# Strassen-form products in six gated tiles of an FFN's up projection, and a later place for the down projection's operands

## The chip, the cores and the metric

The kernel runs on one core of one Trainium2 chip. The metric is the device time of one execution in microseconds (us), as the median of several runs.

## The reference

One layer of a streaming encoder on 544 rows: 512 of a prompt and 32 of a sample. Two attention mixers come first; they and their projections are the same, instruction for instruction, in both kernels. What the change touches is the last line of the layer, the feed-forward part:

```python
# D_MODEL 1024, D_FF 2816, CONV_W 3
x = x + w_down( gelu(a) * b ),  [a | b] = causal depthwise conv3( RMSNorm(x) @ w_up )

u = h @ w_up                                   # h = RMSNorm(x), u has 2*D_FF columns
c = conv_b + conv_w[0]*up[0:t] + conv_w[1]*up[1:1+t] + conv_w[2]*up[2:2+t]
a, g = split(c, 2)
return (gelu(a) * g) @ w_down, up[-(CONV_W-1):]
```

The last two rows of u of prompt and sample are an output, too (the convolution's state).

## The kernel before

**Layout.** Everything is held transposed: features on the 128 partitions, the 544 rows of x as columns. The columns go in two halves of 272 (s = 0 and 1), the 1024 features of x in eight blocks k. For float32 accuracy each operand is split in a high part and a remainder (hi by a rounding copy to fp32r on ScalarE, lo = x - hi on VectorE), and each block product is three matmuls of 128x128 by 272 columns into PSUM: hi by xh, hi by xl, lo by xh. All of them go through one helper, line 86.

**Up projection (the loop over `gate_order`).** w_up has 44 tiles of 128 rows; value tile i and gate tile 22+i make one gated tile, of which there are 22. `conv` does one of the 44: 2 halves by 8 blocks by 3 = 48 matmuls, so 96 a gated tile. Each weight tile (128x1024, 512 KB) is loaded, cast to `w_hi` on ScalarE (L204) and split to `w_lo` on VectorE (L205), three tiles ahead of its use; `w_raw`, `w_hi` and `w_lo` have two buffers each. Behind a half, VectorE multiplies the PSUM sum by the norm's 1/rms and writes it to `u` (L939). Behind the second half GpSimd copies the state's columns, ScalarE starts the convolution (L945), VectorE adds its two other taps (L946, L951), with two small GpSimd instructions between them for the columns where the sample begins. A value tile then gets Gelu (L988, ScalarE), a gate tile is multiplied in (L993, VectorE).

**Operands of the down projection.** The first 6 gated tiles in order (16 to 21, "rest") are split to hi and lo as they are made. The other 16 go in 8 pairs: `make_pair` (L964 to L981) forms sums and differences of the two tiles' halves (VectorE) and splits these. Five of the eight pairs are made between the up projection's tiles, the last three after it.

**Down projection.** The rest part (L1049 to L1061) runs 8 output tiles of 36 matmuls over the 6 rest tiles, each followed by two additions into x1 (L1059). The pair part runs over the pairs, with 7 products of 6 matmuls where the plain form has 8; `sums` makes its weight operands on VectorE (L1018 to L1021, L1025) and ScalarE (L1024), ten ahead.

**Order.** The program is written tile by tile, and a scheduler that simulates a timeline sets each engine's order from it; weight preparation is issued with a priority offset (`LATER`), so that it yields to other ready work. PSUM has eight banks: `psd` with three and `psa` with five, used in turn.

## Time and profile before

| | us |
|---|---|
| median of 3 runs | 921.65 |
| lowest and highest | 920.37, 924.04 |
| the profiled execution | 921.02 |
| its span in the trace | 919.2 |

The span is what the instruction records cover; 1.82 us of the execution lie around it. Busy times are sums of instruction durations. An engine starts its next instruction before the record of the last one ends, so on VectorE and ScalarE the distance from start to start, where rows stand back to back, says what an instruction takes from its engine; the duration is an upper bound. For the matmuls the page's durations overlap, and the distance comes from two events a known number of matmuls apart.

Three stretches of the trace matter: the up projection (from about 531 us, with the norm's factor ready at 543, to 795.6), the rest part (to 831.5) and the pair part (to 916).

### The profile page before, as it was taken

Reading aid. Unit: us, or ns where it says so; the run is one execution under the profiler, and the core shown is the slowest. Engines: PE = TensorE matmul, PEld = TensorE weight load, DVE = VectorE, ACT = ScalarE, POOL = GpSimd, SP = SyncE. Lnnn points to the kernel's source line nnn. Section 1 sums busy time; section 2 is a strip of 40 time slices with the busy share of each in tenths; the row PEclk is TensorE's granted clock in tenths of the full one; section 3 lists DMA queues with packets and bytes.
Section 4 is the critical chain, followed back from the end, with each engine's and each line's share of the span. In section 5 each row is a group of like instructions: output and inputs, shape, how many; then the busy total and the mean of one; then the engine's idle time right before and its main releaser. Section 6 shows DMA issues by size and latency. Waiting matters only on the chain.

```text
span 919.2 us, 18903 instructions
## 1 busy us (share of the span) xinstructions
PE 895.1 (97%) x7085; PEld 881.3 (96%) x7085; DVE 720.0 (78%) x1470; ACT 540.5 (59%) x1283; POOL 378.2 (41%) x577
## 2 busy tenths in 40 slices
PE   7979999999999999999999999999999999999998
PEld 6979999989989999999999999999999999999998
DVE  7798867777988888997856568677787776886996
ACT  5668887778878677777663244334444433534542
POOL 4625548466867767765541213222222221100100
PEclk9999999999999999999999999999999999999999
DMA  7222133312344343343415222222222222232342
GB/s 223 90 89 87 53 96 92 112 58 82 109 133 125 113 145 106 124 126 120 134 47 189 83 79 92 93 92 80 82 93 92 92 90 76 93 107 78 117 146 67
DMA packets 40012, 94.38 MB, mean 103 GB/s; under 512 B 4944, under 2 KB 16240, under 8 KB 39920
## 3 DMA queue, kind: packets, MB, share of 16 engines
q1 hardware_dynamic: 39920, 93.17, 31.9%
q8 instruction: 56, 0.92, 0.4%
q14 instruction: 36, 0.29, 0.1%
HBM read 80.48 MB, written 7.10 MB: 95 GB/s over the span
## 4 chain that ended last, share of the span: by engine, by line
PE 78%; DVE 8%; ACT 3%; POOL 3%; issue 2%; DMA 0%; DVEq 0%; POOLq 0%; ACTq 0%
PE ps L86 75%; PE ps L90 3%; DVE q L449 1%; ACT p L488 1%; DVE w_lo L205 1%; DVE p L504 1%; POOL p L496 1%; DVE zn L425 1%; DVE s L255 1%; DVE t_b L320 1%; POOL t_sql L417 1%; DVE k L434 0%; POOL z L424 0%; DVE xl L328 0%; DMA k<-k 0%
## 5 line engine op out<-in xcount | busy, mean ns | idle before, releaser
L86 PE MATMUL ps<-xh,w_lo 128*128 128x272 f32 x1536 | 445.3, 291 | 5.6 <-DVE w_lo L205 5.6
L86 PE MATMUL ps<-xh,w_hi 128*128 128x272 f32 x1536 | 444.5, 291 | 2.8 <-ACT z L415 1.7
L86 PE MATMUL ps<-xl,w_hi 128*128 128x272 f32 x1536 | 444.5, 290 | 0.4 <-DVE xl L328 0.3
L86 PEld LDWEIGHTS ps<-xh,w_lo 128*128 128x128 f32 x1536 | 290.3, 189 | 7.0 <-DVE w_lo L205 6.5
L86 PEld LDWEIGHTS ps<-xh,w_hi 128*128 128x128 f32 x1536 | 290.1, 189 | 4.6 <-ACT z L415 1.9
L86 PEld LDWEIGHTS ps<-xl,w_hi 128*128 128x128 f32 x1536 | 290.6, 189 | 1.5 <-DVE xl L328 1.1
L205 DVE TENSOR_TENSOR w_lo<-w_raw,w_hi 128x1024 fp32r<-128x1024 f32 (+2 forms) x112 | 143.0, 1277 | 32.6 <-ACT w_hi L204 18.7
L202 POOL TENSOR_SCALAR w_hi<-w_raw 128x1024 fp32r<-128x1024 f32 (+2 forms) x62 | 67.0, 1082 | 92.9 <-PE ps L86 69.2
L496 POOL TENSOR_SCALAR p<-p,rc 128x256 f32<-128x256 f32 (+3 forms) x128 | 74.7, 601 | 41.3 <-DVE rc L494 37.9
L204 ACT CAST w_hi<-w_raw 128x1024 fp32r<-128x1024 f32 x50 | 52.6, 1051 | 64.8 <-issue 36.0
L86 PE MATMUL ps<-s,w_hi 128*128 128x272 f32 x448 | 84.0, 288 | 0.0
L488 ACT ACTIVATE p<-p,nm 128x256 f32<-128x256 f32 (+3 forms) x128 | 65.4, 513 | 28.0 <-DVE nm L485 27.9
L942 POOL TENSOR_SCALAR state_u<-u 128x2 f32<-128x2 f32 x44 | 17.1, 389 | 145.5 <-DVE u L939 145.5
L86 PE MATMUL ps<-s 128*128 128x272 f32 (+1 forms) x483 | 71.3, 293 | 1.7 <-DVE s L374 1.7
L86 PEld LDWEIGHTS ps<-s,w_hi 128*128 128x128 f32 x448 | 70.0, 188 | 0.0
L939 DVE TENSOR_TENSOR u<-ps,rstd 128x272 f32<-128x272 f32 x88 | 38.5, 440 | 39.6 <-PE ps L86 36.9
L86 PEld LDWEIGHTS ps<-s 128*128 128x128 f32 x483 | 65.0, 190 | 2.2 <-DVE s L374 1.7
L86 PE MATMUL ps<-s,w_lo 128*128 128x272 f32 x224 | 63.7, 288 | 0.0
L86 PE MATMUL ps<-k,q 128*128 128x256 f32 (+2 forms) x256 | 52.2, 308 | 3.3 <-DMA k<-k 1.6
L417 POOL TENSOR_TENSOR t_sql<-t_sq,t_sqh 128x272 fp32r<-128x272 f32 x52 | 52.6, 1012 | 3.7
L424 POOL TENSOR_TENSOR z<-z,t_y 128x272 f32<-128x272 f32 x52 | 42.7, 822 | 21.9 <-ACT t_y L317 19.9
L515 DVE TENSOR_TENSOR pt_l<-ps,pt_h 128x512 fp32r<-128x512 f32 (+1 forms) x80 | 45.6, 602 | 5.5 <-ACT pt_h L514 4.3
(164 smaller groups left out, 1627.3 us busy)
## 6 DMA issues: line engine op xcount, KB each, us to landing
w_raw<-in_w_in SPq DMA_DIRECT2D x50, 512.0 KB, 3.4
w_raw<-in_w_up SPq DMA_DIRECT2D x44, 512.0 KB, 3.3
w_raw<-in_w_pair SPq DMA_DIRECT2D x16, 512.0 KB, 3.3
k<-k SPq DMA_DIRECT2D x40, 128.0 KB, 2.3
bias<-in_rel SPq DMA_DIRECT2D x16, 256.0 KB, 2.9
w_raw<-in_w_out SPq DMA_DIRECT2D x8, 512.0 KB, 3.4
s<-in_x SPq DMA_DIRECT2D x15, 272.0 KB, 5.7
w_raw<-in_w_down SPq DMA_DIRECT2D x6, 512.0 KB, 3.3
```

Source lines behind the costliest of these rows:

```text
L86: return self.nc.tensor.matmul(out, lhsT=lhsT, rhs=rhs, **kw)
L90: return self.nc.tensor.transpose(out, src, ident)
L202: G.tensor_scalar(hi[:, c], raw[:, c], 1.0, 1.0, ALU.mult, ALU.mult)
L204: nc.scalar.copy(hi[:, c], raw[:, c])
L205: V.tensor_tensor(lo[:, c], raw[:, c], rr(hi)[:, c], ALU.subtract)
L417: G.tensor_tensor(sql, sq, rr(sqh), ALU.subtract)
L424: G.tensor_tensor(z, z, y, ALU.mult)
L488: act(p[:, sl], p[:, sl], AF.Exp, bias=nm[:, t:t + 1], accum_out=sm[:, t:t + 1])
L496: G.tensor_scalar(p[:, sl], p[:, sl], rc[:, t:t + 1], 1.0, ALU.mult, ALU.mult)
L515: V.tensor_tensor(l[:, :n], ps[:, :n], rr(h)[:, :n], ALU.subtract)
L939: V.tensor_tensor(u[:, 2 + c0:2 + c0 + cn], ps, rstd2[:, c0:c0 + cn], ALU.mult)
L942: G.tensor_scalar(state_u[:, m, 0:2], u[:, NP:NP + 2], 1.0, 1.0, ALU.mult, ALU.mult)
```

## The change

**Shared tiles.** Six of the 22 gated tiles (numbers 7, 9, 11, 13, 15, 17 in the order) no longer run as a value tile and a gate tile. They are taken together as a 2 by 2 product of blocks: {value, gate} by {even blocks k, odd blocks k} by {left half, right half of the columns}. A Strassen form makes it from 7 block products instead of 8. Each is 4 blocks by 3 matmuls = 12, so a shared tile has 84 matmuls for 96. Its weights are four loads of 128x512 (256 KB) in place of two of 512 KB, four sums (VectorE) and seven splits of 128x512 (ScalarE and VectorE). Three products are copied from PSUM on ScalarE and four results are formed on VectorE into the two `u`.

**Rows that carry the norm.** Sums of left and right columns need the factor 1/rms in the rows themselves. So `with_norm` makes scaled rows of x1 (eight, during up tiles 1 to 4), and `form` makes the four sums a pair of blocks needs (during tiles 6 to 9). From up tile 6 on, the plain tiles run on the scaled rows as well, and their sum leaves PSUM by a copy on ScalarE (L960) instead of a multiplication on VectorE.

**Operands later.** The six rest splits, which came tile by tile, come together at gated tile 17; one pair is made after each of the tiles 18 to 21, and the other four in the rest part.

The core of the diff (lines that are left out handle buffers and the host's layout of the weights; the body of `conv_end` is the old code behind `evac`):

```diff
-EARLY = 5
 UNITS = PAIRS // 2
 H = T // 2
+SHARED = (7, 9, 11, 13, 15, 17)
+AHEAD_UP = 6
+TAKE = {17: 6, 18: 1, 19: 1, 20: 1, 21: 1}
 ...
+RESCALE2 = 6
 ...
-    for i in gate_order:
-        sources += [a["w_up"][i], a["w_up"][GT + i]]
+    for n, i in enumerate(gate_order):
+        if n not in SHARED:
+            sources += [a["w_up"][i], a["w_up"][GT + i]]
 ...
+    def conv_end(m, u, done, own):
 ...
+        done(c)
+    def conv(m, n, done, own):
         u = us[n % 2]
 
         def evac(s, c0, cn, ps):
-            V.tensor_tensor(u[:, 2 + c0:2 + c0 + cn], ps, rstd2[:, c0:c0 + cn], ALU.mult)
-            if s == 0:
-                return
 ...
-            done(c)
+            if n < RESCALE2:
+                V.tensor_tensor(u[:, 2 + c0:2 + c0 + cn], ps, rstd2[:, c0:c0 + cn], ALU.mult)
+            else:
+                nc.scalar.copy(u[:, 2 + c0:2 + c0 + cn], ps)
+            if s == 1:
+                conv_end(m, u, done, own)
         dense(evac, psa if n % 2 else psd)
 ...
+    scaled_x, plain, forms = [], [], []
+    def with_norm(k):
+        x = fp.tile([128, T], F32, name="s")
+        V.scalar_tensor_tensor(x, x1[k], col("n2", k), rstd2, ALU.mult, ALU.mult)
+        h, l = (fp.tile([128, T], F32R, name="s") for _ in range(2))
+        split(h, l, x)
+        scaled_x.append(x)
+        plain.append((h, l))
+    def sums_of(v1, v2, t13, t24):
+        b11, b12, b21, b22 = (v[:, c:c + H] for v in (v1, v2) for c in (0, H))
+        V.tensor_tensor(t13[:, :H], b11, b12, ALU.subtract)
+        V.tensor_tensor(t13[:, H:], b12, b22, ALU.subtract)
+        V.tensor_tensor(t24[:, :H], b22, t13[:, :H], ALU.add)
+        V.tensor_tensor(t24[:, H:], b21, t24[:, :H], ALU.subtract)
+    def form(j):
+        t13, t24 = (fp.tile([128, T], F32, name="s") for _ in range(2))
+        sums_of(scaled_x[2 * j], scaled_x[2 * j + 1], t13, t24)
+        ops = {}
+        for e, (names, t) in enumerate(((("t1", "t3"), t13), (("t2", "t4"), t24))):
+            h, l = (xp.tile([128, T], F32R, name=f"x{p}{2 * j + e}") for p in "hl")
+            split(h, l, t)
+            for i, name in enumerate(names):
+                ops[name] = tuple(x[:, i * H:i * H + H] for x in (h, l))
+        for e, names in enumerate((("b11", "b12"), ("b21", "b22"))):
+            for i, name in enumerate(names):
+                ops[name] = tuple(x[:, i * H:i * H + H] for x in plain[2 * j + e])
+        forms.append(ops)
+    def sums_up():
+        for n in range(len(SHARED)):
+            wc, wd, wa, wb = (fp.tile([128, T], F32, name="s")[:, :512] for _ in range(4))
+            for e, w in enumerate((wc, wd, wa, wb)):
+                load(w, a["w_shared"][n, :, 512 * e:512 * e + 512])
+            s1, s2, s3, s4 = (fp.tile([128, T], F32, name="s")[:, :512] for _ in range(4))
+            def both(x):
+                h, l = (fp.tile([128, T], F32R, name="s")[:, :512] for _ in range(2))
+                split(h, l, x)
+                ready_up.append((h, l))
+            both(wa)
+            yield
+            V.tensor_tensor(s1, wc, wd, ALU.add)
+            V.tensor_tensor(s2, s1, wa, ALU.add)
+            both(s2)
+            yield
+            both(s1)
+            yield
+            V.tensor_tensor(s3, wc, wa, ALU.add)
+            both(s3)
+            yield
+            both(wb)
+            yield
+            V.tensor_tensor(s4, s2, wb, ALU.add)
+            both(s4)
+            yield
+            both(wd)
+            yield
+    ready_up, used_up = [], []
 ...
+    def ahead_up(n):
+        while len(ready_up) < len(used_up) + n:
+            with tc.high_priority(LATER):
+                if next(making_up, 0) == 0:
+                    break
+    def shared(m1, m2, nth, done1, done2, own):
+        pool = psa if nth % 2 else psd
 ...
+        ba, bb, bc = (bank(pool)[:, :H] for _ in range(3))
+        p0, q1, e = (ft.tile([128, 272], F32, name=x) for x in ("t_y", "t_b", "t_v"))
+        (y11, y12), (y21, y22) = ((u[:, 2:2 + H], u[:, 2 + H:2 + T]) for u in us)
+        tt = V.tensor_tensor
+        def product(ps, name, first):
+            ahead_up(AHEAD_UP)
+            h, l = ready_up[len(used_up)]
+            used_up.append(name)
+            for j in range(KC // 2):
+                ks = slice(128 * j, 128 * j + 128)
+                xh, xl = forms[j][name]
+                mm(ps, lhsT=h[:, ks], rhs=xh, start=first and j == 0, stop=False, skip_group_check=True)
+                mm(ps, lhsT=h[:, ks], rhs=xl, start=False, stop=False, skip_group_check=True)
+                mm(ps, lhsT=l[:, ks], rhs=xh, start=False, stop=j == KC // 2 - 1, skip_group_check=True)
+        product(bb, "b11", True)
+        nc.scalar.copy(p0, bb)
+        product(ba, "t2", True)
+        nc.scalar.copy(q1, ba)
+        product(bb, "t1", False)
+        nc.scalar.copy(e, bb)
+        product(ba, "t3", False)
+        tt(y22, ba, e, ALU.subtract)
+        product(bc, "b21", True)
+        tt(y11, bc, p0, ALU.add)
+        product(bb, "b22", False)
+        tt(y12, bb, q1, ALU.subtract)
+        conv_end(m1, us[0], done1, own)
+        product(ba, "t4", False)
+        tt(y21, ba, p0, ALU.subtract)
+        conv_end(m2, us[1], done2, fp)
 ...
+    gated, made = [], [0]
+    def take(n):
+        for _ in range(n):
+            j = made[0]
 ...
+            else:
+                j = REST + 2 * (j - REST)
+                if j + 1 >= len(gated):
+                    return
+                make_pair(gated[j], gated[j + 1])
+            made[0] += 1
 ...
+        own = gp if n <= max(SHARED) else fp
 
         def value(c, part=part):
             act(c, c, AF.Gelu)
             part.append(c)
 
-        def gate(c, part=part, n=n):
+        def gate(c, part=part):
             v = part[0]
             V.tensor_tensor(v, v, c, ALU.mult)
-            if n < REST:
-                h, l = home(), home()
-                split(h, l, v)
-                rest.append((h, l))
-                return
-            late.append(v)
-            if n % 2 and len(pairs) < EARLY:
-                make_pair(*late)
-                late.clear()
-        conv(i, 2 * n, value)
-        conv(GT + i, 2 * n + 1, gate)
+            gated.append(v)
+        if n in SHARED:
+            shared(i, GT + i, SHARED.index(n), value, gate, own)
+        else:
+            for e, (m, done) in enumerate(((i, value), (GT + i, gate))):
+                conv(m, tile_no, done, own if e == 0 else fp)
+                if 1 <= tile_no <= 4:
+                    with_norm(2 * tile_no - 2)
+                    with_norm(2 * tile_no - 1)
+                if tile_no == RESCALE2 - 1:
+                    moving[:] = plain
+                if RESCALE2 <= tile_no < RESCALE2 + 4:
+                    form(tile_no - RESCALE2)
+                if tile_no >= RESCALE2 + 4 and len(used_up) < 7 * len(SHARED):
+                    ahead_up(AHEAD_UP)
+                tile_no += 1
+        if n >= max(SHARED):
+            take(TAKE.get(n, 1))
     nc.sync.dma_start(out=o["conv"], in_=state_u)
-    for j in range(0, len(late), 2):
-        make_pair(late[j], late[j + 1])
+    take(GT)
```

What this does to the engines' orders is shown at three places. Names ending in numbers are buffers of one run of the program: `ps` is PSUM, `s` a row buffer, `u0` and `u1` the two inputs of the convolution.

**TensorE where up tile 7 ends.** Up tiles are numbered from 0 here. Before, tile 7 (`w_hi_8415`) ends with its right half; tile 8 (`w_hi_8486`) follows:

```order
L86 MATMUL ps_8584<-xh6_7961,w_hi_8415 128x272
L86 MATMUL ps_8584<-xl6_7962,w_hi_8415 128x272
L86 MATMUL ps_8584<-xh6_7961,w_lo_8416 128x272
L86 MATMUL ps_8584<-xh7_8025,w_hi_8415 128x272
L86 MATMUL ps_8584<-xl7_8026,w_hi_8415 128x272
L86 MATMUL ps_8584<-xh7_8025,w_lo_8416 128x272
L86 MATMUL ps_8629<-xh0_7629,w_hi_8486 128x272 [waits Activation_49]
L86 MATMUL ps_8629<-xl0_7630,w_hi_8486 128x272
L86 MATMUL ps_8629<-xh0_7629,w_lo_8487 128x272 [waits DVE_49]
```

After, tiles 6 (`w_hi_8376`) and 7 (`w_hi_8455`) run together, block by block over four half banks, and end together; tiles 8 (`w_hi_8522`) and 9 (`w_hi_8603`) begin together:

```order
L90 MATMUL ps_8527<-s_8450,w_lo_8377 128x272
L90 MATMUL ps_8553<-s_8451,w_hi_8376 128x272
L90 MATMUL ps_8553<-s_8450,w_lo_8377 128x272
L90 MATMUL ps_8608<-s_8451,w_hi_8455 128x272
L90 MATMUL ps_8608<-s_8450,w_lo_8456 128x272
L90 MATMUL ps_8634<-s_8451,w_hi_8455 128x272
L90 MATMUL ps_8634<-s_8450,w_lo_8456 128x272
L90 MATMUL ps_8689<-s_8207,w_hi_8522 128x272 [waits Activation_49]
L90 MATMUL ps_8689<-s_8208,w_hi_8522 128x272
L90 MATMUL ps_8715<-s_8207,w_hi_8522 128x272
L90 MATMUL ps_8715<-s_8208,w_hi_8522 128x272
L90 MATMUL ps_8770<-s_8207,w_hi_8603 128x272 [waits Activation_49]
```

Both tiles in progress now hold their weight buffers to the end, and two new ones are wanted within ten matmuls.

**ScalarE at the same place.** Before, the casts of tiles 7 to 9 stand between the convolution of earlier tiles:

```order
L204 CAST w_hi_8415<-w_raw_8414 128x1024 [waits DMAHW1_49,PE_49,Activation_49]
L945 ACTIVATE s_8474<-u1_8039,cols_72 128x544 [waits DVE_49]
L433 CAST s_8481<-s_8407 128x544 [waits DVE_49]
L204 CAST w_hi_8486<-w_raw_8485 128x1024 [waits DMAHW2_49,PE_49,Activation_49]
L945 ACTIVATE s_8545<-u0_8038,cols_72 128x544 [waits DVE_49]
L988 ACTIVATE s_8545<-s_8545 128x544 [waits DVE_49]
L204 CAST w_hi_8553<-w_raw_8552 128x1024 [waits DMAHW3_49,PE_49,Activation_49]
```

After, each of the two casts stands behind a copy out of PSUM (L960) that waits for TensorE:

```order
L438 CAST xh0_8594<-s_8588 128x544 [waits DVE_49]
L960 COPY u0_8038<-ps_8527 128x272 [waits PE_49,Activation_49]
L209 CAST w_hi_8522<-w_raw_8521 128x1024 [waits DMAHW2_49,PE_49]
L960 COPY u0_8038<-ps_8553 128x272 [waits PE_49]
L209 CAST w_hi_8603<-w_raw_8602 128x1024 [waits DMAHW3_49,PE_49,Activation_49]
L438 CAST xh1_8598<-s_8589 128x544 [waits DVE_49]
L944 ACTIVATE s_8581<-u0_8038,cols_72 128x544 [waits Activation_49]
```

The two `w_hi` casts follow the last matmuls of tiles 6 and 7 instead of preceding them.

**VectorE around a shared tile.** Before, in the middle of the up projection, one gated tile of the plain kind:

```order
L939 TENSOR_TENSOR u0_8038<-ps_8767,rstd_7626 128x272 [waits PE_49]
L951 SCALAR_TENSOR_TENSOR s_8750<-u1_8039,cols_72,s_8750 128x544 [waits DVE_49,Pool_49]
L993 TENSOR_TENSOR s_8683<-s_8683,s_8750 128x544 [waits DVE_49]
L939 TENSOR_TENSOR u0_8038<-ps_8793,rstd_7626 128x272 [waits PE_49]
L434 TENSOR_TENSOR s_8758<-s_8683,s_8757 128x544 [waits Activation_49]
L205 TENSOR_TENSOR w_lo_8763<-w_raw_8761,w_hi_8762 128x1024 [waits DMAHW6_49,Activation_49]
L946 SCALAR_TENSOR_TENSOR s_8821<-u0_8038,cols_72,s_8821 128x544 [waits Activation_49]
L939 TENSOR_TENSOR u1_8039<-ps_8834,rstd_7626 128x272 [waits PE_49]
L951 SCALAR_TENSOR_TENSOR s_8821<-u0_8038,cols_72,s_8821 128x544 [waits DVE_49,Pool_49]
```

After, the end of the second shared tile, with the sums and splits of the third one's weights between its four results (the four results are those that read `ps`):

```order
L1065 TENSOR_TENSOR u0_8038<-ps_9448,t_y_9449 128x272 [waits PE_49,Activation_49]
L1128 TENSOR_TENSOR s_9367<-s_9367,s_9439 128x544 [waits DVE_49]
L439 TENSOR_TENSOR s_9495<-s_9484,s_9494 128x512 [waits DMAHW6_49,Activation_49]
L1012 TENSOR_TENSOR s_9490<-s_9482,s_9483 128x512 [waits DMAHW5_49,DMAHW4_49]
L1013 TENSOR_TENSOR s_9491<-s_9490,s_9484 128x512 [waits DVE_49]
L1063 TENSOR_TENSOR u1_8039<-ps_9446,t_v_9451 128x272 [waits PE_49,Activation_49]
L439 TENSOR_TENSOR s_9514<-s_9491,s_9513 128x512 [waits Activation_49]
L439 TENSOR_TENSOR s_9531<-s_9490,s_9530 128x512 [waits Activation_49]
L1018 TENSOR_TENSOR s_9492<-s_9482,s_9484 128x512
L1067 TENSOR_TENSOR u0_8038<-ps_9447,t_b_9450 128x272 [waits PE_49]
L439 TENSOR_TENSOR s_9549<-s_9492,s_9548 128x512 [waits Activation_49]
L1070 TENSOR_TENSOR u1_8039<-ps_9446,t_y_9449 128x272 [waits PE_49]
```

The multiplications by 1/rms are gone; splits of 128x512 and the four results stand in their place.

**VectorE at the end of the rest part.** Before, with the first weight operand of the pair part (`s_11523`) made after the additions of the fifth output tile (`s_7614`):

```order
L1059 TENSOR_TENSOR s_7614<-ps_11390,s_7614 128x272 [waits PE_49]
L1059 TENSOR_TENSOR s_7614<-ps_11391,s_7614 128x272 [waits PE_49]
L1018 TENSOR_TENSOR s_11518<-w_raw_11516 128x512 [waits DMAHW5_49]
L1020 TENSOR_TENSOR s_11519<-s_11518,w_raw_11516 128x256 [waits DVE_49]
L205 TENSOR_TENSOR w_lo_11394<-w_raw_11392,w_hi_11393 128x1024 [waits DMAHW4_49,PE_49,Activation_49]
L1021 TENSOR_TENSOR s_11519<-s_11519,w_raw_11516 128x256 [waits DVE_49]
L1025 TENSOR_TENSOR s_11523<-w_raw_11516,s_11523 128x256 [waits Activation_49]
L1025 TENSOR_TENSOR s_11526<-s_11519,s_11526 128x256 [waits Activation_49]
L1025 TENSOR_TENSOR s_11529<-s_11518,s_11529 128x256 [waits Activation_49]
```

After, the last pair's differences (L982) and splits (L439) stand ahead of it, and the first weight operand (`s_11777`) comes after the additions of the seventh (`s_7616`):

```order
L981 TENSOR_TENSOR s_11446<-s_11286,s_11445 128x272 [waits DVE_49]
L1200 TENSOR_TENSOR s_7616<-ps_11730,s_7616 128x272 [waits PE_49]
L982 TENSOR_TENSOR s_11446<-s_11286,s_11446 128x272 [waits DVE_49]
L1200 TENSOR_TENSOR s_7616<-ps_11731,s_7616 128x272 [waits PE_49]
L439 TENSOR_TENSOR s_11451<-s_11445,s_11450 128x544 [waits Activation_49]
L439 TENSOR_TENSOR s_11453<-s_11446,s_11452 128x544 [waits Activation_49]
L1159 TENSOR_TENSOR s_11772<-w_raw_11770 128x512 [waits DMAHW1_49]
L1161 TENSOR_TENSOR s_11773<-s_11772,w_raw_11770 128x256 [waits DVE_49]
L1166 TENSOR_TENSOR s_11777<-w_raw_11770,s_11777 128x256 [waits Activation_49]
L1162 TENSOR_TENSOR s_11773<-s_11773,w_raw_11770 128x256 [waits DVE_49]
L1166 TENSOR_TENSOR s_11780<-s_11773,s_11780 128x256 [waits Activation_49]
```

The making of pairs has moved between the additions, and the first weight operand two output tiles later.

## Rows read from the trace of the kernel before

**Rows 1.** The page: busy time, share of the span, instructions of each engine.
```profile
PE 895.1 (97%) x7085; PEld 881.3 (96%) x7085; DVE 720.0 (78%) x1470; ACT 540.5 (59%) x1283; POOL 378.2 (41%) x577
```
**Rows 2.** Windows (us): length, busy of PE, PEld, DVE, ACT, POOL, clock, DMA, GB/s.
```profile
300.00:400.00 100.00, 97.02 (x757) 93.80 (x757) 88.95 (x182) 74.75 (x209) 72.13 (x86) 1.00 0.41 124
543.00:795.60 252.60, 252.60 (x2019) 252.60 (x2018) 190.00 (x289) 109.46 (x142) 63.41 (x172) 1.00 0.27 90
795.60:831.50 35.90, 35.90 (x288) 35.90 (x288) 28.62 (x58) 12.52 (x21) 2.23 (x4) 1.00 0.28 91
831.50:916.00 84.50, 84.38 (x674) 84.16 (x673) 71.03 (x185) 39.30 (x109) 7.30 (x8) 1.00 0.31 104
```
**Rows 3.** The chain that ended last, by time: start, length, what.
```profile
475.21 440.69 PE ps L86 x3510
```
**Rows 4.** VectorE timeline, up projection: start, duration, instruction, idle before and its end.
```profile
567.12 0.44 DVE L939 TENSOR_TENSOR u<-ps,rstd 128x272 f32<-128x272 f32 x1 [1.26 <-PE ps L86]
...
573.13 0.44 DVE L939 TENSOR_TENSOR u<-ps,rstd 128x272 f32<-128x272 f32 x1 [0.92 <-PE ps L86]
...
784.60 1.23 DVE L205 TENSOR_TENSOR w_lo<-w_raw,w_hi 128x1024 fp32r<-128x1024 f32 x1 [0.56 <-ACT w_hi L204]
785.74 0.78 DVE L946 SCALAR_TENSOR_TENSOR s<-u,cols,s 128x544 f32<-128x544 f32 x1
...
793.16 0.79 DVE L951 SCALAR_TENSOR_TENSOR s<-u,cols,s 128x544 f32<-128x544 f32 x1
793.86 0.72 DVE L434 TENSOR_TENSOR xh<-s,xl 128x544 fp32r<-128x544 f32 x1
794.50 0.44 DVE L969 TENSOR_TENSOR xh<-s,xh 128x272 fp32r<-128x272 f32 x1
794.85 0.44 DVE L969 TENSOR_TENSOR xl<-s,xl 128x272 fp32r<-128x272 f32 x1
```
**Rows 5.** VectorE groups from 800 us: line, tile, count, busy, mean ns, idle before.
```profile
L1025 DVE TENSOR_TENSOR s<-s 128x256 fp32r<-128x256 f32 x64 | 25.5, 426 | 3.0 <-ACT s L1024 3.0
...
L1018 DVE TENSOR_TENSOR s<-w_raw 128x512 f32<-128x512 f32 x16 | 10.9, 684 | 1.7 <-DMA w_raw<-in_w_pair 1.7
```
**Rows 6.** VectorE groups from 535 to 800 us, the same columns.
```profile
L939 DVE TENSOR_TENSOR u<-ps,rstd 128x272 f32<-128x272 f32 x88 | 38.5, 440 | 39.6 <-PE ps L86 36.9
```
**Rows 7.** ScalarE timeline, end of the up projection.
```profile
794.88 0.63 ACT L433 CAST xh<-s 128x544 fp32r<-128x544 f32 x1
795.54 1.05 ACT L204 CAST w_hi<-w_raw 128x1024 fp32r<-128x1024 f32 x1
796.50 0.41 ACT L968 CAST xh<-s 128x272 fp32r<-128x272 f32 x1
796.81 0.84 ACT L945 ACTIVATE s<-u,cols 128x544 f32<-128x544 f32 x1
```
**Rows 8.** ScalarE groups from 535 to 800 us.
```profile
L204 ACT CAST w_hi<-w_raw 128x1024 fp32r<-128x1024 f32 x44 | 46.2, 1051 | 48.8 <-PE ps L86 25.0 <-issue 23.7
```
**Rows 9.** ScalarE groups from 800 us.
```profile
L1081 ACT COPY t_y<-ps 128x272 f32<-128x272 f32 x4 | 1.5, 387 | 6.8 <-PE ps L86 6.8
```
**Rows 10.** The page: DMA issues, KB each, median us from issue to landing.
```profile
w_raw<-in_w_up SPq DMA_DIRECT2D x44, 512.0 KB, 3.3
...
bias<-in_rel SPq DMA_DIRECT2D x16, 256.0 KB, 2.9
```
**Rows 11.** VectorE timeline where the pair part begins.
```profile
831.39 0.82 DVE L1059 TENSOR_TENSOR s<-ps,s 128x272 f32<-128x272 f32 x2 [3.40 <-PE ps L86]
```
**Rows 12.** ScalarE timeline where the pair part begins.
```profile
832.52 0.41 ACT L1024 CAST s<-w_raw 128x256 fp32r<-128x256 f32 x1 [9.69 <-PE ps L86]
```

More of the change, by code (lines that the diff above doesn't have):

```diff
@@ L936, in conv @@
+    def conv(m, n, done, own):
         u = us[n % 2]
         def evac(s, c0, cn, ps):
-            V.tensor_tensor(u[:, 2 + c0:2 + c0 + cn], ps, rstd2[:, c0:c0 + cn], ALU.mult)
-            if s == 0:
-                return
-            G.tensor_scalar(state_u[:, m, 0:2], u[:, NP:NP + 2], 1.0, 1.0, ALU.mult, ALU.mult)
-            G.tensor_scalar(state_u[:, m, 2:4], u[:, T:T + 2], 1.0, 1.0, ALU.mult, ALU.mult)
-            c = fp.tile([128, T], F32, name="s")
-            act(c, u[:, 0:T], AF.Identity, scale=col("cw0", m), bias=col("cb", m))
@@ L957, in body @@
     rest, pairs = [], []
-    homes = [gp] * 19 + [fp] * (7 * EARLY + 2 * REST - 19) + [f"x{p}{k}" for k in range(KC) for p in "hl"]
+    homes = [f"x{p}{k}" for k in range(KC) for p in "hl"] + HOMES(gp, fp)
     def home():
@@ L970, in make_pair @@
         split(*wide[0], v2)
-        V.tensor_tensor(t13[:, :H], b11, b12, ALU.subtract)
-        V.tensor_tensor(t13[:, H:], b12, b22, ALU.subtract)
+        sums_of(v1, v2, t13, t24)
         split(*wide[1], t13)
-        V.tensor_tensor(t24[:, :H], b22, t13[:, :H], ALU.add)
-        V.tensor_tensor(t24[:, H:], b21, t24[:, :H], ALU.subtract)
         split(*wide[2], t24)
@@ L981, in make_pair @@
         pairs.append(ops)
-    late = []
+    gated, made = [], [0]
+    def take(n):
+        for _ in range(n):
+            j = made[0]
+            if j < REST:
+                if j >= len(gated):
+                    return
+                h, l = home(), home()
+                split(h, l, gated[j])
+                rest.append((h, l))
+            else:
+                j = REST + 2 * (j - REST)
+                if j + 1 >= len(gated):
+                    return
+                make_pair(gated[j], gated[j + 1])
+            made[0] += 1
+    tile_no = 0
     for n, i in enumerate(gate_order):
         part = []
+        own = gp if n <= max(SHARED) else fp
         def value(c, part=part):
@@ L1134, in _layout @@
     r["w_up"] = _tiles(f["w_up"][0])
+    up = r["w_up"].reshape(2, GT, 128, KC // 2, 2, 128)
+    order = list(range(2 * PAIRS, GT)) + [j + e * PAIRS for j in range(PAIRS) for e in range(2)]
+    r["w_shared"] = np.ascontiguousarray(
+        up[::-1][:, [order[n] for n in SHARED]].transpose(1, 2, 0, 4, 3, 5).reshape(len(SHARED), 128, 2048))
     wd = _tiles(f["w_down"][0]).reshape(KC, 128, GT, 128)
```

17 lines of the change are left out of this document (11 added, 6 removed).

## The prediction, made before the changed kernel ran

> **What bounds the kernel now.** The page has TensorE busy for 97% of the span, VectorE for 78% [rows 1]. Next I read the chain of waits: its last long link is TensorE alone, from 475.21 us for 440.69 us without one wait [rows 3]. The whole feed-forward part lies in it. Then the windows: TensorE is busy for all 252.60 us of the up projection, all of the rest part, and 84.38 of 84.50 us of the pair part [rows 2]. So the time there is matmuls times the distance between them. Two first-half evacuations of neighbouring up tiles start at 567.12 and 573.13 [rows 4]; 48 matmuls lie between: 6.01 us / 48 = **125.2 ns**. (The durations of matmul records overlap and can't be used.) VectorE is next: 190.0 us busy by durations in the up projection, 75% [rows 2], and much of its idle time there is waiting for TensorE (39.6 us ahead of L939) [rows 6]. Whether the change pays is then one question: does TensorE stay without gaps with fewer matmuls and more VectorE work?
>
> **What instructions take.** On VectorE I go from start to start where rows stand back to back [rows 4]: 128x1024 remainder 1.14 us (784.60 to 785.74), 128x544 with a scalar column 0.70 (793.16 to 793.86), 128x544 plain 0.64 (to 794.50), 128x272 0.35 (to 794.85). The durations are 0.09 us longer. 128x512 has no such pair: between 0.61 (from 0.35 and 0.64 by length) and its duration, 0.684 [rows 5]. On ScalarE a weight cast is 1.05 us long (the mean of 44) [rows 8], 0.96 to the next start [rows 7], and a 128x272 copy out of PSUM 0.387 [rows 9].
>
> **The saving.** Six tiles at 84 matmuls for 96 are 72 fewer, and the order after has just these fewer. 72 x 125.2 ns = **-9.01 us**, if TensorE is fed. The two-row products, the scaled rows and the later operands add no matmul. The Trainium skill (TensorE: Matmul & The Clock Gate, Back-to-back issue gap) gives N/2.4 + 2.5 ns for an isolated warm matmul, an estimate of 115.8 ns for 272 columns and 8.3 us for 72; the row says 125.2, and the measurement decides.
>
> **VectorE as a whole.** Counted in the order from the norm's factor to the end of the up projection, after: 94 x 0.70 + 68 x 0.35 + 66 of 128x512 x 0.65 + 53 x 0.64 + 31 x 1.14 = 202 us, of 252.6 - 9.0 = 243.6 us: 83%. Before: 86 x 0.70 + 114 x 0.35 + 44 x 0.64 + 42 x 1.14 = 176 of 252.6, 70%. The multiplications by 1/rms (0.35 each) go to ScalarE as copies (0.39 each), which has room: 109.46 of 252.60 us busy [rows 2]. In a plain tile with a shared one, 180 matmuls or 22.5 us, VectorE has 5.7 us for the plain tile (2 x 1.14 + 4 x 0.70 + 0.64) and 11.5 to 12.3 for the shared one (11 x 0.61 to 0.684, 4 x 0.35, 4 x 0.70, 0.64): 77 to 80%. It is not the bound; what can cost is a place where something is late.
>
> **Place 1, up tiles 7 to 9.** The scaled rows are made by VectorE during tiles 1 to 5, block by block, and TensorE runs tiles 6 and 7 together as the blocks arrive. By the counts the last block's remainder is ready at about 575.5 us and wanted at 577.6, so no loss there. But both tiles end together, with both buffers of `w_hi` held until then. Before, the next cast ran while 48 matmuls of the other tile were left. Now ScalarE's queue at that place is copy, cast, copy, cast; the first copy waits for the last matmul of tile 6's left half. Behind that moment TensorE has 6 matmuls (0.75 us) and then wants a cast that comes after 0.39 + 1.05 = 1.44 us; it gets 4 matmuls (0.50) and wants the second, another 1.44 us later. Loss: 2 x 1.44 - 10 x 0.125 = **1.6 us**. With the starts' distances (0.31 and 0.96) it is 1.3; with some delay at each hand-over 2.0. I take 1.6, since on ScalarE each step waits for the end of another engine's. Queued behind the waiting copy are just these casts, and TensorE waits for them.
>
> **Place 2, shared tiles.** Product t1 adds into the bank that b11 left, and t3 into t2's, so each waits for a copy (p0, q1); b22 waits for the copy e, t4 for VectorE's y22. The order puts matmuls of other products and of the next plain tile between: 24 to 37, 3.0 to 4.6 us, against a copy of 0.39 that may stand behind one cast (1.05) and a 0.84 us convolution [rows 7], 2.3 us. On VectorE y22 may stand behind a 1.14 and two 0.64: 2.8 us with its own. Enough, by a little. Nothing excludes small losses: 0 to 0.1 us a tile, **+0.3** in all; the upper bound is a rival below. The weights: 6 x 4 loads of 256 KB are 24 new transfers for 12 of 512 KB that go. A load of 256 KB lands in 2.9 us [rows 10]. They are issued about 13.2 us ahead of use, a plain tile and some of the shared one; four one after another would take 11.6. Covered; the DMA share was 0.27 there [rows 2].
>
> **Place 3, end of the rest part.** The rest splits at tile 17 and the pairs move, and the last pairs' work now lies in the rest part: some 29.6 us of VectorE by starts in 36.05 us of matmuls. The second additions of the seventh output tile can't start before 31.3 us into it; behind them stand a difference, two splits, the first operand's sums and its remainder, 3.8 us by starts and 4.3 by durations, so the operand is ready at 35.1 to 35.6 and wanted at 36.3. Before there was far more room: ScalarE stood idle for 9.69 us and VectorE for 3.40 at that point [rows 11, 12]. After that an operand takes VectorE 0.53 us and TensorE's 6 matmuls 0.75. From 0 to 1.5 us (the chain a hand-over late at each of five steps); I take **+0.2**. By the Trainium skill (VectorE: DVE Perf Modes, The DRAIN you can't avoid) the next instruction of the engine begins only when the pipe has run empty. The rows don't bear it out here: starts lie 0.35 us apart at 0.44 us of duration [rows 4]. By the rule VectorE would need the durations instead, 225 us of 243.6 in the up projection, and this place would lose its 1.5 us: 915.4 in all.
>
> **Sum.** 921.02 (the profiled execution: 919.2 of span and 1.82 around it) - 9.01 + 1.6 + 0.3 + 0.2 = **914.1 us**. The median of 3 is 0.6 above that execution, so I don't read this closer than 0.6.
>
> **The clock** was granted at 1.00 in all four windows, full speed, 2.4 GHz, and also between 300 and 400 us where TensorE was busy for 97.02 of 100 us in pieces [rows 2]. Stalls of 1 to 2 us should leave it there.
>
> **Rivals.**
> 1. *Everything hidden.* The copies and casts at place 1 overlap better than I count, and the other places lose nothing: 921.02 - 9.01 = 912.0. For it: TensorE had no gap in 440 us. Against: place 1 follows from the order with durations of rows alone.
> 2. *Each shared tile leaks.* The margins of place 2 were counted with one instruction in front. With a state copy or a second cast more in front (0.4 to 1.05 us), the copy or y22 comes 0.4 to 0.9 us late, say 0.7 in each of six tiles: +4.2, and 1.5 at the end of the rest part: 921.02 - 9.01 + 1.6 + 4.2 + 1.5 = 919.3, not to be told from no change. For it: three ScalarE copies and four VectorE results a tile now gate TensorE, where two evacuations a tile gated nothing. Against: ScalarE is under half busy.
> 3. *Slower: the weights of the shared tiles come late.* SyncE's queue holds the four loads until the previous shared tile's buffers are free, and everything behind (four sums, seven casts, seven remainders) waits in a row. If the four land one after another at over 3.3 us each, 13.2 us are used up and TensorE waits. At 4.0 us each it is 16.0 - 13.2 = 2.8 us in each of five tiles, 14 in all: 914.1 + 14 = 928. It is slower than before from 3.8 us each (over 2.4 us lost a tile). For it: a 512 KB weight took 3.3 us and 256 KB 2.9 [rows 10], so smaller loads are hardly quicker. Against: loads at 90 GB/s with a share of 0.27 [rows 2] run side by side.
> 4. *It doesn't do what it says.* The matmuls in the order are 72 fewer; I give this nothing.
>
> **How the numbers follow.** Forecast, 912.5 to 917: 0.57. Rival 1, about 912: 0.11. Rival 2 and milder forms of 3, 917 to 920.5: 0.20. Between there and 926.3: 0.04. Rival 3, over 926.3: 0.08. About 0.5% (4.6 us) is what a measurement can tell from no change, so faster is below 917.0 and slower above 926.3: 0.68, 0.24, 0.08. The range leaves out the slower cases and little else: 911.5 to 920.0, from 0.5 below rival 1 to 0.7 above rival 2 (the 0.6 between execution and median).
>
> **What would show it.** Right: the link of TensorE in the chain is broken once near 577 us, with two idle times of 0.7 to 1 us that a cast from L209 ends; plain tiles stay at 6.01 us, a plain with a shared tile at 22.5; the idle time of TensorE ahead of the first pair product is below 0.5 us; windows show VectorE at about 88% by durations in the up projection. Wrong: idle times of TensorE inside shared tiles that a copy (L1057, L1059, L1061) or y22 (L1063) ends (rival 2), or that a remainder behind a DMA ends (rival 3); VectorE without idle time anywhere; a granted clock under 1.00.

## The result, and the profile after

The changed kernel took 914.76 us (median of 4 runs, 913.71 to 915.08) against 921.58 us for the kernel before; the ratio is 0.9922 with a 95% interval of 0.9904 to 0.9941, so it is 0.8% faster. The profiled execution took 914.91 us with a span of 913.1. Two more comparisons on other chips gave 0.9916 (0.9902 to 0.9929) and 0.9927 (0.9915 to 0.9939).

The page of the changed kernel, busy time of each engine, beside [rows 1]:

```profile
PE 888.1 (97%) x7013; PEld 872.7 (96%) x7013; DVE 743.7 (81%) x1512; ACT 582.4 (64%) x1399; POOL 421.0 (46%) x577
```

TensorE has 72 matmuls fewer (7013 for 7085) and 7.0 us less busy time. The chain that ended last, beside [rows 3] (start, length, what):

```profile
476.38 103.81 PE ps L90 x821
582.26 325.98 PE ps L90 x2600
```

The one long link is broken once, between 580.19 and 582.26 us. The list of TensorE's waits from 470 us on has a single line (what it waited for: us in total, times, longest):

```profile
PE ps L90 <- ACT w_hi L209: 1.2, 2, 0.7
```

The windows of the three stretches, with the columns of [rows 2]; the first is the up projection, then the rest part and the pair part:

```profile
544.20:789.30 245.10, 243.91 (x1943) 243.40 (x1943) 205.10 (x314) 144.63 (x245) 105.78 (x172) 1.00 0.29 93
789.30:825.20 35.90, 35.90 (x290) 35.90 (x290) 33.23 (x67) 17.45 (x31) 2.42 (x5) 1.00 0.24 79
825.20:909.70 84.50, 84.50 (x675) 84.31 (x673) 73.51 (x192) 40.35 (x113) 7.32 (x8) 1.00 0.33 108
```

TensorE idles for 1.2 us in the first and nowhere else. VectorE's share rose from 75% to 84% there and from 80% to 93% in the rest part.

**A measure that scatters less than the whole time.** The long link starts at 475.21 us before and at 476.38 after, although everything ahead of it is the same: 1.2 us of scatter in the unchanged part. So below I compare the *stretch* from the start of this link to the last copy of a product out of PSUM in the pair part (`t_y`, L1081 before, L1222 after), which waits for TensorE. It is 911.46 - 475.21 = 436.25 us before, and 905.31 - 476.38 = 428.93 after; the changed kernel's other two profiles gave 429.20 and 428.91. The difference is **-7.32 us**; the kernel before was profiled once.

| kernel | ratio to before (95%) | stretch, us |
|---|---|---|
| before | 1 | 436.25 |
| changed (three profiles) | 0.9922, 0.9916, 0.9927 | 428.93, 429.20, 428.91 |
| e_r8, e_r8b: scaled rows from tile 8 | 0.9900 (0.9885-0.9914), 0.9905 (0.9890-0.9919) | 427.37, 427.38 |
| e_sh0: nothing shared | 1.0022 (1.0012-1.0031) | 438.56 |
| e_copy2: copies twice | 0.9911 (0.9896-0.9926) | 429.13 |
| e_ah2: operands two products ahead | 0.9921 (0.9908-0.9933) | 429.27 |
| e_dma2: weights loaded twice | 1.0042 (1.0027-1.0058) | 439.96 |
| e_sh16: 7 shared, three in a row | 0.9912 (0.9899-0.9924) | 429.36 |
| e_pairs: 7 shared, two pairs | 0.9951 (0.9937-0.9964) | 430.93 |
| e_sh7: 7 shared, from tile 5 | 0.9972 (0.9961-0.9984) | 433.67 |
| e_sh8: 8 shared | 0.9986 (0.9976-0.9997) | 434.94 |

### The profile page after: what moved, and what is told of

Its sections match the earlier page's. It is cut to its first block, busy times and chain, and to the rows that moved or that the text cites. A ratio compares the mean times of both kernels' runs of the same rounds, so it can differ in the third digit from the quotient of the medians.

```text
span 913.1 us, 18964 instructions
## 1 busy us (share of the span) xinstructions
PE 888.1 (97%) x7013; PEld 872.7 (96%) x7013; DVE 743.7 (81%) x1512; ACT 582.4 (64%) x1399; POOL 421.0 (46%) x577
## 4 chain that ended last, share of the span: by engine, by line
PE 76%; DVE 9%; ACT 4%; POOL 4%; issue 2%; DVEq 0%; POOLq 0%; ACTq 0%
PE ps L90 73%; PE ps L94 3%; DVE q L454 1%; DVE zn L430 1%; ACT p L493 1%; DVE p L509 1%; POOL p L501 1%; DVE w_lo L210 1%; POOL t_sql L422 1%; POOL z L429 1%; DVE t_b L325 1%; DVE k L439 1%; POOL s L707 0%; POOL t_sqh L421 0%; DVE pt_l L520 0%
## 5 line engine op out<-in xcount | busy, mean ns | idle before, releaser
L90 PE MATMUL ps<-xh,w_lo 128*128 128x272 f32 x1024 | 297.5, 292 | 5.9 <-DVE w_lo L210 5.9
L90 PE MATMUL ps<-xh,w_hi 128*128 128x272 f32 x1024 | 297.5, 293 | 1.9 <-ACT z L420 1.7
L90 PE MATMUL ps<-xl,w_hi 128*128 128x272 f32 x1024 | 297.8, 292 | 0.3 <-DVE xl L333 0.3
L90 PE MATMUL ps<-s,w_hi 128*128 128x272 f32 x1088 | 205.3, 288 | 1.2 <-ACT w_hi L209 1.2
L90 PEld LDWEIGHTS ps<-xh,w_lo 128*128 128x128 f32 x1024 | 194.2, 190 | 7.2 <-DVE w_lo L210 6.7
L90 PEld LDWEIGHTS ps<-xh,w_hi 128*128 128x128 f32 x1024 | 193.9, 190 | 4.3 <-ACT z L420 2.0
L90 PEld LDWEIGHTS ps<-xl,w_hi 128*128 128x128 f32 x1024 | 194.5, 190 | 1.3 <-DVE xl L333 0.7
L90 PEld LDWEIGHTS ps<-s,w_hi 128*128 128x128 f32 x1088 | 169.9, 188 | 1.6 <-ACT w_hi L209 1.6
L90 PE MATMUL ps<-s,w_lo 128*128 128x272 f32 x544 | 154.1, 287 | 0.0
L210 DVE TENSOR_TENSOR w_lo<-w_raw,w_hi 128x1024 fp32r<-128x1024 f32 (+2 forms) x100 | 128.3, 1283 | 27.0 <-POOL w_hi L207 13.9
L90 PEld LDWEIGHTS ps<-s,w_lo 128*128 128x128 f32 x544 | 101.8, 188 | 0.1
L941 POOL TENSOR_SCALAR state_u<-u 128x2 f32<-128x2 f32 x44 | 30.3, 689 | 118.0 <-ACT u L960 41.1
L209 ACT CAST w_hi<-w_raw 128x1024 fp32r<-128x1024 f32 x38 | 40.0, 1053 | 44.6 <-PE ps L90 29.7
L439 DVE TENSOR_TENSOR s<-s 128x512 fp32r<-128x512 f32 (+1 forms) x80 | 55.7, 710 | 2.2 <-ACT s L438 2.1
```

The costliest lines, as they stand in the source:

```text
L90: return self.nc.tensor.matmul(out, lhsT=lhsT, rhs=rhs, **kw)
L209: nc.scalar.copy(hi[:, c], raw[:, c])
L210: V.tensor_tensor(lo[:, c], raw[:, c], rr(hi)[:, c], ALU.subtract)
L439: e.tensor_tensor(dst_lo, src, rr(dst_hi), ALU.subtract)
L941: G.tensor_scalar(state_u[:, m, 0:2], u[:, NP:NP + 2], 1.0, 1.0, ALU.mult, ALU.mult)
```

## The experiments

The theory was the prediction's: 72 matmuls at 125.2 ns are saved, 1.6 us are lost where up tiles 6 and 7 end together, and the shared tiles themselves lose next to nothing (0.3 allowed in all).

### Place 1: the two tiles that end together

TensorE's timeline of the changed kernel there (start, duration, instruction, count, idle before):

```profile
580.02 0.28 PE L90 MATMUL ps<-s,w_lo 128*128 128x272 f32 x1
581.02 0.77 PE L90 MATMUL ps<-s,w_hi 128*128 128x272 f32 x4 [0.72 <-ACT w_hi L209]
582.26 0.76 PE L90 MATMUL ps<-s,w_hi 128*128 128x272 f32 x4 [0.47 <-ACT w_hi L209]
582.88 0.40 PE L90 MATMUL ps<-s,w_lo 128*128 128x272 f32 x1
583.11 0.42 PE L90 MATMUL ps<-s,w_hi 128*128 128x272 f32 x2
583.36 0.29 PE L90 MATMUL ps<-s,w_lo 128*128 128x272 f32 x1
```

From the matmul at 580.02 to the one at 583.36 there are 12 distances, 1.50 us at 125.2 ns; it took 3.34. The loss is 1.84 us, more than the two idle times of 0.72 and 0.47, since a record's modelled end hides the first part of a gap. By the starts it is 0.88 us ahead of 581.02, 0.74 from there to 582.26, and 0.22 behind that. ScalarE beside it:

```profile
579.64 0.39 ACT L960 COPY u<-ps 128x272 f32<-128x272 f32 x1 [0.26 <-PE ps L90]
579.92 1.05 ACT L209 CAST w_hi<-w_raw 128x1024 fp32r<-128x1024 f32 x1
580.87 0.39 ACT L960 COPY u<-ps 128x272 f32<-128x272 f32 x1
581.15 1.06 ACT L209 CAST w_hi<-w_raw 128x1024 fp32r<-128x1024 f32 x1
```

Copy, cast, copy, cast, as the order had it, and TensorE starts 0.05 us behind each cast's end. The last 0.22 us are not ScalarE's alone: the first matmul that reads a remainder starts at 582.88, 0.05 us behind the end of VectorE's split.

```profile
581.61 1.22 DVE L210 TENSOR_TENSOR w_lo<-w_raw,w_hi 128x1024 fp32r<-128x1024 f32 x1
```

To undo this place, the scaled rows come two tiles later, when all of them are ready. This takes away the common end of the two tiles and the copies ahead of the casts at once (VectorE evacuates tiles 6 and 7 again); the run can't tell these two apart:

```diff
-RESCALE2 = 6
+RESCALE2 = 8
```

> One number changed: the scaled rows are taken up from up tile 8 on instead of 6, and the sums of columns are formed two tiles later. All eight scaled rows are then ready when the first tile wants them, so tiles 7 to 9 run one after another. Theory (the 1.84 us that TensorE lost between 580.0 and 583.4 us come from two tiles ending together with all weight buffers held): no idle time of TensorE there, 914.8 - 1.8 = 912.9 us. Rival (the loss only moves: the forms come two tiles later and the first shared tile waits for them): an idle time of TensorE near 615 us and 914 to 915 us.

Measured: 0.9900, and the list of TensorE's waits in this stretch is empty. The chain has no gap near 580 us any more (477.57 + 142.31 = 619.88):

```profile
477.57 142.31 PE ps L90 x1128
619.89 285.72 PE ps L90 x2280
```

The stretch is 427.37 us, 1.56 less than the changed kernel's. A small part of the loss did move, to where the rival had it: at the first shared tile TensorE starts a plain tile's matmul late, behind a remainder that VectorE ends at 619.83.

```profile
619.60 0.29 PE L90 MATMUL ps<-xl,s 128*128 128x272 f32 x1
619.89 0.39 PE L90 MATMUL ps<-s,w_lo 128*128 128x272 f32 x1
620.12 0.41 PE L90 MATMUL ps<-s,w_hi 128*128 128x272 f32 x2
```

```profile
618.61 1.22 DVE L210 TENSOR_TENSOR w_lo<-w_raw,w_hi 128x1024 fp32r<-128x1024 f32 x1 [0.84 <-ACT w_hi L209]
```

Two distances take 0.52 us there for 0.25, so 0.27 us of the 1.84 are lost again, and 1.57 are left. Since the two totals came from different chips, the changed kernel ran once more beside other runs (e_after), and then both beside each other on one chip (e_after2 and e_r8b):

```diff
 (no edit: the changed kernel itself)
```

> The changed kernel once more, on the chip of the next three. 0.9922 of the kernel before, with the same 1.2 us of idle time of TensorE (1.84 us lost) near 580 us into the execution and no other.

> The changed kernel beside the next two, for a comparison on one chip: 0.992 of the kernel before, TensorE idle for 1.2 us near 580 us.

> Scaled rows from up tile 8 on, again, beside the changed kernel on one chip. By the first look's trace the feed-forward stretch is 1.55 us shorter than in the changed kernel: 1.5 to 1.9 us less, ratio to the kernel before 0.990. Rival (the first comparison was scatter between chips): 0.992, no difference.

Measured: 0.9916 and 0.9927 for the changed kernel, 0.9905 for scaled rows from tile 8 on; 915.98 and 913.80 us as medians of the two on one chip, stretches 428.91 and 427.38. So 1.5 us of the place are real, and e_r8 is the fastest kernel of this study in both of its comparisons. The intervals of the ratios (0.9915 to 0.9939 and 0.9890 to 0.9919) still touch; what separates the two is the stretch, which repeats within 0.3 us.

### Place 2: what the shared tiles cost themselves

```diff
+SHARING = ()
-        if n not in SHARED:
+        if n not in SHARING:
...
-        if n in SHARED:
+        if n in SHARING:
```

> No tile is shared: all 22 gated tiles run as 96 matmuls, with everything else of the change kept (scaled rows, copies on ScalarE from tile 6 on, the down projection's operands made later). Theory (the shared tiles save 72 x 125.2 ns = 9.0 us and lose nothing): 914.8 + 9.0 = 923.8 us, that is 2.2 above the kernel before. Rival (each shared tile leaks 0.3 us, hidden in the pace of the records): 914.8 + 9.0 - 1.8 = 922.0.

Measured: 1.0022 and a stretch of 438.56 us, 9.5 us more than the changed kernel's mean of 429.0 (the theory: 9.0; the rival: 7.2). The shared tiles leak nothing. The 0.5 above the theory lie outside of them. A part is place 1, which costs more in e_sh0 than in the changed kernel:

```profile
584.77 0.77 PE L91 MATMUL ps<-s,w_hi 128*128 128x272 f32 x4 [0.47 <-ACT w_hi L210]
585.61 0.39 PE L91 MATMUL ps<-s,w_lo 128*128 128x272 f32 x1
```

These four distances take 0.84 us, the same ones in the changed kernel 0.62 (582.26 to 582.88). The rest is the pace of plain tiles. In e_sh0, two evacuations that wait for TensorE, 21 tiles apart, and two of the kernel before, 36 tiles apart:

```profile
618.00 0.39 ACT L961 COPY u<-ps 128x272 f32<-128x272 f32 x1 [0.34 <-PE ps L91]
...
744.56 0.39 ACT L961 COPY u<-ps 128x272 f32<-128x272 f32 x1 [0.94 <-PE ps L91]
```

```profile
579.14 0.44 DVE L939 TENSOR_TENSOR u<-ps,rstd 128x272 f32<-128x272 f32 x1 [1.68 <-PE ps L86]
...
795.62 0.44 DVE L939 TENSOR_TENSOR u<-ps,rstd 128x272 f32<-128x272 f32 x1 [0.33 <-PE ps L86]
```

126.56 / 21 = 6.027 us a plain tile, against 216.48 / 36 = 6.013. So a plain tile on the scaled rows is 0.2% slower, without an idle time; why is open. The changed kernel's own plain tiles are as slow where two stand in a row (12.05 us for two), but a plain with a shared tile is not:

```profile
762.59 0.39 ACT L960 COPY u<-ps 128x272 f32<-128x272 f32 x1 [0.93 <-PE ps L90]
...
774.64 0.39 ACT L960 COPY u<-ps 128x272 f32<-128x272 f32 x1 [0.20 <-PE ps L90]
```

```profile
652.99 0.44 DVE L1067 TENSOR_TENSOR u<-ps,t_b 128x272 f32<-128x272 f32 x1 [0.70 <-PE ps L90]
...
675.53 0.44 DVE L1067 TENSOR_TENSOR u<-ps,t_b 128x272 f32<-128x272 f32 x1 [0.69 <-PE ps L90]
```

That is 22.54 us for 180 matmuls, 125.2 ns each.

Two runs then took from the margins. First each of the three copies twice:

```diff
         nc.scalar.copy(p0, bb)
+        nc.scalar.copy(p0, bb)
...
         nc.scalar.copy(q1, ba)
+        nc.scalar.copy(q1, ba)
...
         nc.scalar.copy(e, bb)
+        nc.scalar.copy(e, bb)
```

> In each shared tile the three copies out of PSUM on ScalarE (p0, q1, e) are made twice, 0.39 us more each. Theory (24 or more matmuls stand between a product and the one that waits for its copy, 3.0 us against some 1.2 us that copy and queue take): no idle time in the shared tiles, 914.8 us, within 0.5. Rival (the copies are at their edge): up to 3 x 0.39 us in each of six tiles, 7 us, 918 to 922 with idle times that these copies end.

Measured: 0.9911, a stretch of 429.13 us, and the same single line in the list of waits. The copies are not at their edge: 0.39 us more for each fit. Then less lead in the written order:

```diff
-AHEAD_UP = 6
+AHEAD_UP = 2
```

> The shared tiles' weight operands are ordered two products ahead of their use instead of six (3 us for 9); loads stand in the same order. Theory (the order's lead is not what keeps TensorE fed, the engines run ahead as far as buffers allow): within 0.7 us of the changed kernel. Rival (the lead is what hides VectorE's sums and splits): over 1 us in each shared tile, 6 us or more, with idle times of TensorE ended by casts or remainders of 128x512.

Measured: 0.9921, 429.27 us, one further wait of 0.2 us. The lead as written decides nothing here.

### The weights of the shared tiles

The page of the changed kernel, DMA issues (KB each, median us to landing), beside [rows 10], and SyncE's timeline (start, time from the first issue to the last's end, count):

```profile
s<-in_w_shared SPq DMA_DIRECT2D x24, 256.0 KB, 4.2
```

```profile
630.59 1.75 SPq L174 DMA_DIRECT2D s<-in_w_shared  x4
...
651.72 3.59 SPq L174 DMA_DIRECT2D s<-in_w_shared  x4
```

A load takes 4.2 us to land, not the 2.9 that I took from another tensor's 256 KB, but the four are issued within 1.8 to 3.6 us and overlap. To see what it would cost if they didn't, each load is issued twice:

```diff
                 load(w, a["w_shared"][n, :, 512 * e:512 * e + 512])
+                load(w, a["w_shared"][n, :, 512 * e:512 * e + 512])
```

> Each load of a shared tile's weights is issued twice, 48 transfers of 256 KB instead of 24. They are issued some 13 us before use. Theory (the loads run side by side: they landed in 4.2 us each in the changed kernel without TensorE waiting): eight land within about 8 us, no idle time of TensorE in the shared tiles, 914.8 us within 0.7. Rival (one after another, 8 x 4.2 = 34 us): the first sums come over 10 us late in each of at least four tiles, 940 us or more. In between (the queue of SyncE holds the next plain weights back by the four issues): up to 1.5 us a tile, 915 to 922.

Measured: 926.98 us, 1.0042, slower than before; a stretch of 439.96, 11 us more than the changed kernel's. None of the three expectations had it, and the timeline says why: the second load of a buffer waits for the first to land, so the eight are issued one after another, and SyncE's queue holds the next plain weights back behind them.

```profile
597.13 16.95 SPq L174 DMA_DIRECT2D s<-in_w_shared  x8
614.13 7.85 SPq L174 DMA_DIRECT2D w_raw<-in_w_up  x3
```

TensorE then waits for a plain tile's cast first (1.72 us at 620.42 us, on `w_hi` of L209). So this run did not double the traffic on parallel paths; it made the loads serial, as in the prediction's third rival, for 15.3 to 17.6 us at all but the last tile. The price is below the rival's: 11.0 us over the changed kernel by the stretch, for the 14 that it gave to 16 us of loading (the totals, 926.98 and 928, don't compare: the kernel before took 923.18 on that chip and 921.58 on the first). And only a part goes the rival's way. TensorE waited 2.7 us in all for casts of the shared tiles' operands, but the longest waits are for a plain tile's cast and, with 2.0 us, for the first operand of the pair part.

### How many shared tiles

If a shared tile costs nothing, more of them should pay. With the scaled rows from tile 8 on:

```diff
-SHARED = (7, 9, 11, 13, 15, 17)
+SHARED = (7, 9, 11, 13, 15, 16, 17)
-RESCALE2 = 6
+RESCALE2 = 8
```

> Scaled rows from up tile 8 on (no tiles that end together), and gated tile 16 shared as well: seven shared tiles, three of them (15, 16, 17) in a row. 12 matmuls fewer, 1.5 us. Theory (VectorE has room on the whole, and six products, 9 us, of lead absorb a short row): the changed kernel - 1.84 - 1.5, a ratio to the kernel before of 0.9886. Rival (VectorE decides where shared tiles are neighbours: 3 x 11.5 to 12.3 us of its work against 3 x 10.5 of TensorE's, 3 to 5 us short): 2 to 4 us lost again, ratio 0.991 to 0.993, with idle times of TensorE that remainders of VectorE or casts end.

```diff
-SHARED = (7, 9, 11, 13, 15, 17)
+SHARED = (7, 9, 10, 12, 13, 15, 16, 17)
-RESCALE2 = 6
+RESCALE2 = 8
```

> Scaled rows from up tile 8 on, and eight shared tiles: 7, 9, 10, 12, 13, 15, 16, 17. 24 matmuls fewer than the changed kernel, 3.0 us; VectorE's work in the up projection 214 us of 240.6. Theory: the changed kernel - 1.84 - 3.0, ratio 0.987. Rival (neighbouring shared tiles wait for VectorE or for their weights, 1 to 3 us at each of three places): ratio 0.990 to 0.997.

Measured: the rivals in both, e_sh8 past its range. e_sh16 has a stretch of 429.36 us, 2.0 more than e_r8 in spite of 1.5 us of matmuls less; TensorE waits 1.2 us for a remainder of 128x512 and 1.0 for a cast. e_sh8 is only 1.3 us shorter than the kernel before. Its TensorE and VectorE at the worst place:

```profile
722.85 0.57 PE L90 MATMUL ps<-xh,s 128*128 128x272 f32 x1 [6.59 <-DVE u L1063]
```

```profile
719.90 0.78 DVE L950 SCALAR_TENSOR_TENSOR s<-u,cols,s 128x544 f32<-128x544 f32 x1 [0.25 <-POOL s L948]
720.93 0.78 DVE L950 SCALAR_TENSOR_TENSOR s<-u,cols,s 128x544 f32<-128x544 f32 x1 [0.25 <-POOL s L948]
721.63 0.72 DVE L1128 TENSOR_TENSOR s<-s 128x544 f32<-128x544 f32 x1
722.27 0.43 DVE L1063 TENSOR_TENSOR u<-ps,t_v 128x272 f32<-128x272 f32 x1
```

The result y22 (L1063), which product t4 waits for, stands on VectorE behind the convolutions of both halves of the tile before, and two of their steps wait 0.25 us each for GpSimd. Behind the 6.59 us the granted clock was 0.50 from 723 to 727 us, which costs again. Two more ways to place a seventh tile: alternating, but two tiles sooner,

```diff
-SHARED = (7, 9, 11, 13, 15, 17)
+SHARED = (5, 7, 9, 11, 13, 15, 17)
```

> Gated tile 5 shared as well, seven shared tiles that alternate with plain ones (5, 7, ... 17), scaled rows from up tile 6 on as in the changed kernel. 12 matmuls fewer. Theory (shared tiles pay wherever a plain tile follows them): the changed kernel - 1.5, ratio 0.9900. Rival (the first shared tile now stands directly behind the forming of the sums of columns, and its weights are fetched while VectorE was busy for 36.0 of 38.8 us): TensorE waits for its operands for 2 us or more there, ratio 0.992 to 0.996.

and neighbours in pairs only:

```diff
-SHARED = (7, 9, 11, 13, 15, 17)
+SHARED = (7, 9, 11, 12, 14, 16, 17)
-RESCALE2 = 6
+RESCALE2 = 8
```

> Scaled rows from up tile 8 on, and seven shared tiles with neighbours in pairs, none in threes: 7, 9, 11, 12, 14, 16, 17. 12 matmuls fewer than with six. Theory (VectorE's shortage and the waiting of GpSimd's small instructions add up over a row of shared tiles, and a plain tile behind each pair makes it good): with three in a row 3.5 us were lost against six spread ones; with pairs at most 0.7 a pair, so the feed-forward stretch is 427.4 - 1.5 + 1.4 = 427.3 us or less, ratio to the kernel before 0.989 to 0.990. Rival (each neighbouring tile costs what it saves and more, since TensorE waits for results that stand behind two convolutions on VectorE): over 429 us, ratio 0.993 or more.

Measured: the rivals again, e_sh7 past its range: 433.67 us (6.2 lost against 427.5) and 430.93 us (5.0 lost against 425.9). The longest wait of e_pairs, 1.71 us at 745.44, is for a result of VectorE (L1065), the kind of wait that its rival named. In e_sh7 the loss lies ahead of the first shared tile, where VectorE makes the sums of columns and of the weights at once: TensorE waits 1.40 us for a cast and 2.07 us for a remainder of plain weights.

```profile
595.05 0.77 PE L90 MATMUL ps<-s,w_hi 128*128 128x272 f32 x4 [1.40 <-ACT w_hi L209]
597.89 0.41 PE L90 MATMUL ps<-s,w_lo 128*128 128x272 f32 x1 [2.07 <-DVE w_lo L210]
```

So of the orders tried, none with seven or eight beats six, each with a plain tile behind it. Seven that alternate, with scaled rows from tile 8 on, and other orders of the same instructions were not tried.

## Why the prediction was right, step by step

- **The saving.** 72 fewer matmuls at 125.2 ns: the distance held (22.54 us for 180), and e_sh0 gives 9.5 us against 9.01, where 0.2 are e_sh0's dearer place 1 and the slower plain tiles are the rest as far as is known. They take 6.025 to 6.027 us where the forecast had 6.01. (The two evacuations from which I took the 125.2 ns are of second halves, not of first ones as the text has it; the distance is the same.)
- **Place 1, +1.6.** The mechanism was right: 1.84 us by the timeline, 1.56 by undoing it. That 1.6 came so close is in part luck. The first wait cost 0.88 for 0.69, as the copy started 0.25 us behind the last matmul's slot, a hand-over that the 1.6 left out; the second cost 0.74 for 0.94, as ScalarE's copy and cast followed each other by starts (0.28 and 0.95 us) and only the cast that TensorE waits for counts in full; and the 0.22 behind the second cast, with VectorE's remainder, were not in the sum. The idle records are 0.72 and 0.47 near 580 us, where the text looked for two of 0.7 to 1 near 577. The rows of the last block came in time, as counted: tiles 6 and 7 ended with the offset of the unchanged part and no idle time.
- **Place 2, +0.3.** Nothing. The 0.3 was an allowance that no row gave, and e_copy2 shows 0.39 us of room or more at each copy, which the count (3.0 us against 2.3) allowed.
- **The weights.** The price of a load was mis-sized, 4.2 us side by side for 2.9; one after another, in e_dma2, the median was 3.4, so four in a row would have been 13.6 us and not 11.6, just past the 13.2 us of lead. The step held because the loads overlap, which the text had as the reason against the rival, not in the sum.
- **Place 3, +0.2.** Nothing. VectorE's timeline from the seventh output tile's first addition to the first operand's remainder:

```profile
820.70 0.44 DVE L1200 TENSOR_TENSOR s<-ps,s 128x272 f32<-128x272 f32 x1 [0.50 <-PE ps L90]
...
824.09 0.42 DVE L1166 TENSOR_TENSOR s<-w_raw,s 128x256 fp32r<-128x256 f32 x1
```

  It ends at 824.51, 3.8 us after 820.70, as worked out by starts. The pair part's first three matmuls are these:

```profile
825.35 0.54 PE L90 MATMUL ps<-xh,s 128*128 128x272 f32 x3
```

  The third, 0.25 us behind the first, wants it at 825.60. 1.1 us are left, 0.7 to 1.2 by the forecast; of the 3.40 us of idle time before [rows 11] nothing is. The +0.2 was an allowance, too.
- **VectorE's load.** 205.10 of 245.10 us by durations, 84%; I had said about 88%.
- **The sum.** 921.02 - 9.01 + 2.1 = 914.1, the profiled execution 914.91. In the stretch alone it was -6.91 forecast and -7.32 measured; the 1.2 us by which the unchanged part came later hides that the forecast was 0.4 us too careful. Of the 0.4, the allowances not needed give 0.5 and the dearer place 1 takes 0.2; the last 0.1 is within what the stretch scatters.
- **The clock.** Right here, 1.00 in all windows, but the reason was too wide: see below.

## What to carry to other kernels

On a path that one engine holds without gaps, the forecast is instructions saved by the distance of two events in the trace, minus what the order shows at each place where two things now end at once; durations across engines, start distances within one. Look for such places first, since undoing one (RESCALE2 = 8) gave 1.5 us more, while a seventh tile, in the three orders tried, lost more to waits for VectorE and ScalarE than it saved. Measure over a stretch that holds only what changed: for the two kernels profiled more than once it repeated within 0.3 us, where whole executions of one kernel scattered by up to 5.
